# The last three groups of a gated MLP: down projections kept in PSUM, two more 4 KB places, loads spread out

## The chip, the cores and the metric

The kernel runs on one core of one Trainium2 chip. The metric is the device time of one execution in microseconds (us), by the median of several runs; less is better. All data is float32, and nearly all work is done on TensorE (PE in the profile), which multiplies a 128x128 stationary block by a moving block of up to 512 columns into PSUM. VectorE is DVE, ScalarE is ACT, GpSimd is POOL and SyncE is SP; PEld is the loading of stationary blocks, which overlaps PE.

## The reference, cut to what matters

A trunk of two layers over 256 positions of width 2048. Each layer is an attention mixer and then a gated MLP (the FFN) with a width of 5632 and a causal convolution of width 3 on the gate. The change touches the end of both FFNs.

```python
def _conv_ffn(h, w_up, w_conv, b_conv, w_down):
    u = h @ w_up
    gate, val = jnp.split(u, 2, axis=-1)
    gp = jnp.pad(gate, ((0, 0), (CONV_WIDTH - 1, 0), (0, 0)))
    acc = b_conv + gp[:, CONV_WIDTH - 1:CONV_WIDTH - 1 + S] * w_conv[CONV_WIDTH - 1]
    for j in range(CONV_WIDTH - 1):
        acc = acc + gp[:, j:j + S] * w_conv[j]
    return (jax.nn.silu(acc) * val) @ w_down

def _finish_layer(x, heads, w_o, norms, w_up, w_conv, b_conv, w_down):
    x = x + _rmsnorm(heads @ w_o, norms[1])
    f = _conv_ffn(_rmsnorm(x, norms[2]), w_up, w_conv, b_conv, w_down)
    return x + _rmsnorm(f, norms[3])
```

The output is x after both layers, 256 x 2048.

## The kernel before

**Numbers in two parts.** Every weight block of 128 x 2048 (1 MB, tile `raw`, three buffers) is loaded by an SP DMA in `piece` and split into a rounded part (`whi`, ACT, L557) and the rest (`wlo`, DVE, L558), four half-blocks of each. `mm3` (L118) forms a product by three matmuls: high by high, low by high, high by low.

**The FFN.** Its 5632 columns are eleven groups of 512. Groups 2, 4, 6 and 8 are "wide": `wide` uses a scheme of seven products with sums of weight blocks, which DVE makes in `sums` (d at L590, e at L591 and L592). The others are "narrow": sixteen-step products (`ws_tile`, L135 to L140), four such tiles for each pair of 256 columns, eight for a group. `keep` puts the activations of a group into two places of the pool `sh`. That pool has nine places of 4 KB per partition; it also holds d and e, the results of the down projections (y), loaded quarters of the memory tokens, and, through the whole FFN of layer 0, the memory keys of layer 1.

**Down projections.** A group's activations times `w_down` give four chunks of 512 columns (c = 0..3). `down(g, c)` loads one weight block, does 24 matmuls (12 for each half t of the positions) into a bank with tag "s", lets ACT copy each half to a place of `sh` (L701), and POOL sends it to `yout` in device memory, adding to what is there (L687 the first time, L689 later). Inside `wide`, one such down stands in each of the eight units of the loop, for the two groups before. After the last wide group (8), groups 9 and 10 are made; then eight downs follow for groups 8 and 9; then `yout` is read back into four places of `sh` (L788, `ys`). The eleventh group (g = 10) is done in PSUM: `evac` adds it to `ys` (L792), squares it (ACT, L205) and multiplies it by the gain (L796); when c = 3 is through, `rstd` follows (L198 on DVE, L200 on POOL), and `add_normed` adds four chunks to x (L489). In layer 1 the eleventh group runs half by half: all c for t = 0, then all c for t = 1, with the weights held in `h1` and `h2`; then SP stores the output (L978). In layer 0 it runs chunk by chunk, and `filler` (the values of memory for layer 1) follows.

**What sets the order.** `later(n, fn)` puts work into a list; each `ws_tile` and each `as_piece` takes one entry off (`step`). Below that the Tile layer schedules instructions of each engine and puts DMAs into the queue of the engine that issues them; a queue is in order, and an instruction waits there for its place in a pool to be free. The residual x is read back from device memory after the last wide group (L774, on POOL), and in layer 0 `late()` (`again` in `run`) also loads the four quarters of the memory tokens (`load_T`: SP at L248, then ACT L229 and DVE L230 four times each).

Of the kernel before, what the change touches and what calls it, by code (L numbers as in the profile page):

```python
# [30 lines left out]
COL_G = {"a0": 0, "a2": 16, "a4": 32, "b0": 48, "b2": 64, "b4": 80, "kv": 96}  # L31
# [4 lines left out]
GROUPS = DFF // 512  # L36
# [9 lines left out]
class Body:  # L46
# [16 lines left out]
        return self.sb.tile(shape, F32, name="sc", tag="sc", bufs=4)  # L63

    def sh(self, shape, dtype=F32):
        return self.sb.tile(shape, dtype, name="sh", tag="sh", bufs=9)

    def pairtile(self, dtype=F32):
        return self.sb.tile([P, 2, S], dtype, name="qk", tag="qk", bufs=5)
# [587 lines left out]
    def ffn(self, layer, h, each, filler=None, done=None, late=None):  # L657
        nc = self.nc
        up, uw, dn = (self.a["%s%d" % (k, layer)] for k in ("up", "uw", "dn"))
# [23 lines left out]
        acts = {}  # L683

        def out(g, c, part):
            if g == 0:
                nc.gpsimd.dma_start(yout[c], part)  # L687
            else:
                nc.gpsimd.dma_start(yout[c], part, accum_op=ALU.add)  # L689

        def down(g, c):


            parts = self.piece(dn[c, g])
            y = self.sh([P, 1024])
            yield
            for t in range(2):
                b = self.bank("s")
                self.as_mm([b, b], parts, acts[g], 0, (t,))
                yield  # L700
                self.pin(nc.scalar.copy(y[:, t * 512:(t + 1) * 512], b))  # L701
                if t:
                    out(g, c, y)
                else:
                    yield
# [29 lines left out]
        def narrow(g):  # L735
            for p in (2 * g, 2 * g + 1):
                w = p - 2 * sum(v < g for v in WIDE)
                ga = self.ws_pair(up[w, 0], h)
                if p == 0:

                    val = self.ws_pair(up[w, 1], h)
                Rb = spread().unsqueeze(1).to_broadcast([P, 2, S])
                nc.vector.tensor_tensor(ga, ga, Rb, op=ALU.mult)
                c = conv(p, ga)
                nc.vector.tensor_tensor(c, c, Rb, op=ALU.mult)
                if p:
                    val = self.ws_pair(up[w, 1], h)
                keep(p, c, val)

        def turned(g, made, i):  # L750

            both = []
            for of in made:
                b = self.bank("s")
                for j in range(2):
                    for t in range(2):
                        f = (2 * i + j) * P
                        nc.tensor.transpose(b[:, j * S + t * P:j * S + (t + 1) * P], of[t][:, f:f + P], self.ident)
                both.append(b.rearrange("p (j t) -> p j t", j=2))
            keep(2 * g + i, conv(2 * g + i, both[0]), both[1])  # L760
# [3 lines left out]
        before = [0, 1]  # L764
        forms = self.sb.tile([P, 4, 1024], F32R, name="x", tag="x", bufs=1)
        for g in WIDE:
            downs = [lambda b=b, c=c: down(b, c) for b in before for c in range(4)]
            made = self.wide(uw[WIDE.index(g)], h, s, forms, R[0], downs)
            for i in range(2):
                self.later(2 + i, lambda made=made, g=g, i=i: turned(g, made, i))  # L770
            if g == WIDE[-1]:
                self.x = self.sb.tile([P, 2, D], F32, name="x", tag="x", bufs=1)
                for t in range(2):
                    nc.gpsimd.dma_start(self.x[:, t, :], self.xout[t])  # L774
                if late:
                    late()
            narrow(g + 1)
            before = [g, g + 1]
        narrow(GROUPS - 1)
        for b in before:  # L780
            for c in range(4):
                for _ in down(b, c):
                    pass
        g = GROUPS - 1
        gs = [self.gain(2 * layer + 1, c) for c in range(4)]
        ys = [self.sh([P, 2, 512]) for _ in range(4)]
        for c in range(4):
# [2 lines left out]
        def evac(c, t, b):  # L790
            y = ys[c][:, t, :]
            nc.vector.tensor_add(y, y, b)  # L792
            self.square_into(y, ss[:, t, c:c + 1])
            if c == 3:
                r[t] = self.rstd(ss[:, t:t + 1, :])
            nc.vector.tensor_tensor(y, y, gs[c], op=ALU.mult)  # L796

        if not filler:

            banks = [[self.bank(), self.bank()] for _ in range(2)]  # L800
            banks += [[self.bank("s"), self.bank("s")] for _ in range(2)]
            store = self.stores("h1") + self.stores("h2")
            parts = [self.piece(dn[c, g], store=store[c]) for c in range(4)]
            for t in range(2):
                for c in range(4):
                    self.as_mm(banks[c], parts[c], acts[g], 0, (t,))
                    evac(c, t, banks[c][t])
                self.add_normed(ys, r[t], t, lambda c: done(t, c))
            return
        for c in range(4):  # L810
            b = self.as_chunk(dn[c, g:], acts[g])
            for t in range(2):
                evac(c, t, b[t])
        self.add_normed(ys, r[0], 0)
# [4 lines left out]
    def run(self):  # L819
        nc, a = self.nc, self.a  # L820
# [22 lines left out]
        b = self.bank("s")  # L843
# [65 lines left out]
        for j in range(12):  # L909
# [5 lines left out]
            if j % 3 == 2:  # L915
                i = j // 3
# [4 lines left out]
        lhs = [(mh[:, i, :], ml[:, i, :]) for i in range(4)] + [(dh[:, i, :], dl[:, i, :]) for i in range(4)]  # L921
# [11 lines left out]
        def again():  # L933
            self.memT = self.hset("h1")
            for i in range(4):
                self.load_T(a["memT"], COL_G["b4"], self.memT, i)

        self.ffn(0, h, lambda c: self.x_T(COL_G["kv"], hk, [c]), lambda: res.update(mv=self.mem_v(1)), late=again)
        mk, mv = res["mk"], res["mv"]

# [13 lines left out]
        def outs(hh):  # L954
            return heads[hh // 4][0][:, hh % 4, :], heads[hh // 4][1][:, hh % 4, :]
# [7 lines left out]
        hh, hl, _ = self.hset("h1")  # L963
        heads[2] = (hh[:, 0:4, :], hl[:, 0:4, :])
        lhs = [(mh[:, i, :], ml[:, i, :]) for i in range(4)] + [outs(i) for i in range(12)]
# [93 lines left out]

# [13 lines left out]
```

## Time and profile before

| | |
|---|---|
| runs | 2220.97 us median of 3 (2219.81 to 2222.61) |
| the profiled execution | 2222.25 us, of which the program's span is 2220.5 us |
| PE busy | 2190.2 us, 99% of the span, 11106 matmuls |
| PEld, DVE, ACT, POOL busy | 83%, 77%, 59%, 4% |
| granted TensorE clock | 9 tenths or more in all forty slices but the last (8) |
| moved by DMA | 479.04 MB, 216 GB/s in the mean |

In a row of the timeline stand the start, the duration, the engine, the line, the operation, the tiles and the count of merged instructions; in square brackets the idle time of the engine before it and what ended it. Matmuls are pipelined: one of 512 columns lasts 0.39 us in a row, and the next begins 0.23 us after it. So PE counts as busy nearly always, and what it loses stands in its few brackets.

### The profile page before, as it was taken

To read this page: it belongs to the slowest core of one execution; us is meant where nothing else is said; L and a number is where in the kernel's file an instruction comes from. 1 tells how busy PE (TensorE), PEld (TensorE's weight loads), DVE (VectorE), ACT (ScalarE), POOL (GpSimd) and SP (SyncE) were. 2 spreads that over 40 slices of the span, in tenths; PEclk is the share of its full clock that TensorE was granted. 3 is DMA by queue.
4 is the path that set the end of the run, shared out by engine and by line. 5 is a ranking of instruction groups with operands and counts; after the bars stand their busy time and mean duration, and the time that the engine had idled before them with its cause. 6 is when DMAs were issued, how large, how long until landed. Compare 5 with 4: busy or idle time off the path is not lost. (4 is left out here: it accounts for less than half of the span.)

```text
span 2220.5 us, 29136 instructions
## 1 busy us (share of the span) xinstructions
PE 2190.2 (99%) x11106; PEld 1846.8 (83%) x11106; DVE 1708.9 (77%) x2215; ACT 1313.2 (59%) x1870; POOL 93.8 (4%) x138
## 2 busy tenths in 40 slices
PE   9999999999999999999999999999999999999996
PEld 7888888888888888888788888878888888888885
DVE  6566767888888888886574677569989889898755
ACT  7545656566666666665564554456666666666553
POOL 0000000000000000000100000000000000000001
PEclk9999999999999999999999999999999999999998
DMA  8754555558586776875945444555676868778676
GB/s 321 267 178 159 196 182 210 182 207 262 194 252 198 245 229 208 272 259 192 282 172 190 152 171 168 193 190 190 236 237 199 254 192 256 218 231 259 227 214 187
DMA packets 76012, 479.04 MB, mean 216 GB/s; under 512 B 8672, under 2 KB 9056, under 8 KB 25312
## 3 DMA queue, kind: packets, MB, share of 16 engines
q1 hardware_dynamic: 60768, 418.45, 54.3%
q0 software_dynamic: 15104, 58.73, 11.7%
q8 instruction: 87, 1.43, 0.3%
q14 instruction: 53, 0.43, 0.1%
HBM read 428.91 MB, written 48.23 MB: 215 GB/s over the span
## 5 line engine op out<-in xcount | busy, mean ns | idle before, releaser
L558 DVE TENSOR_TENSOR wlo<-raw,whi 128x1024 fp32r<-128x1024 f32 (+1 forms) x758 | 879.3, 1174 | 324.7 <-ACT whi L557 313.7
L557 ACT CAST whi<-raw 128x1024 fp32r<-128x1024 f32 (+1 forms) x758 | 760.1, 1012 | 362.6 <-PE ps_g L118 132.9
L135 PE MATMUL ps_g<-h,whi 128*128 128x512 f32 x2640 | 942.4, 399 | 1.9 <-ACT whi L557 1.7
L136 PE MATMUL ps_g<-h,wlo 128*128 128x256 f32 x2816 | 760.7, 280 | 0.7 <-DVE wlo L558 0.7
L135 PEld LDWEIGHTS ps_g<-h,whi 128*128 128x128 f32 x2640 | 495.7, 188 | 116.3 <-ACT whi L557 2.2
L136 PEld LDWEIGHTS ps_g<-h,wlo 128*128 128x128 f32 x2816 | 531.3, 189 | 15.3 <-DVE wlo L558 1.0
L118 PE MATMUL ps_s<-whi,sh 128*128 128x512 f32 x1280 | 396.1, 391 | 0.0
L118 PEld LDWEIGHTS ps_s<-whi,sh 128*128 128x128 f32 x1280 | 240.4, 188 | 52.7
L118 PE MATMUL ps_s<-wlo,sh 128*128 128x512 f32 x640 | 252.3, 394 | 4.0 <-DVE wlo L558 4.0
L118 PE MATMUL ps_g<-whi,h 128*128 128x512 f32 x816 | 254.1, 392 | 0.8 <-ACT whi L557 0.8
L139 ACT COPY qk<-ps_g 128x256 f32<-128x256 f32 x160 | 59.6, 372 | 210.9 <-PE ps_g L138 210.8
L118 PEld LDWEIGHTS ps_g<-whi,h 128*128 128x128 f32 x816 | 152.7, 188 | 34.7 <-ACT whi L557 1.3
L701 ACT COPY sh<-ps_s 128x512 f32<-128x512 f32 x160 | 93.2, 582 | 130.3 <-PE ps_s L118 118.6
L558 DVE TENSOR_TENSOR x<-sh,x 128x1024 fp32r<-128x1024 f32 x128 | 156.0, 1222 | 15.8 <-ACT x L557 9.6
L118 PE MATMUL ps_g<-wlo,h 128*128 128x512 f32 x408 | 160.1, 393 | 0.2
L118 PEld LDWEIGHTS ps_s<-wlo,sh 128*128 128x128 f32 x640 | 120.2, 188 | 32.5 <-DVE wlo L558 6.5
L557 ACT CAST x<-sh 128x1024 fp32r<-128x1024 f32 x128 | 134.3, 1050 | 17.8 <-PE ps_s L118 16.4
L118 PE MATMUL ps_g<-whi,sh 128*128 128x512 f32 x368 | 115.5, 395 | 0.7 <-ACT whi L557 0.7
L140 DVE TENSOR_TENSOR qk<-ps_g,qk 128x256 f32<-128x256 f32 x160 | 67.3, 421 | 57.0 <-ACT qk L139 56.2
L118 PE MATMUL ps_g<-x,h 128*128 128x512 f32 x384 | 109.2, 392 | 0.0
L118 PE MATMUL ps_s<-x,h 128*128 128x512 f32 x384 | 108.5, 391 | 0.0
L689 POOL DMA_DIRECT2D yout<-sh x72 | 61.5, 855 | 1044.8 <-ACT sh L701 1034.5
(173 smaller groups left out, 1920.0 us busy)
## 6 DMA issues: line engine op xcount, KB each, us to landing
raw<-in_up_dram SPq DMA_DIRECT2D x112, 1024.0 KB, 4.9
raw<-in_dn_dram SPq DMA_DIRECT2D x88, 1024.0 KB, 4.9
raw<-in_uw_dram SPq DMA_DIRECT2D x64, 1024.0 KB, 7.1
yout<-sh POOLq DMA_DIRECT2D x80, 512.0 KB, 8.4
raw<-in_wqk_a_dram SPq DMA_DIRECT2D x24, 1024.0 KB, 4.9
raw<-in_wo_b_dram SPq DMA_DIRECT2D x16, 1024.0 KB, 4.9
raw<-in_wv_a_dram SPq DMA_DIRECT2D x12, 1024.0 KB, 4.8
raw<-in_wv_b_dram SPq DMA_DIRECT2D x12, 1024.0 KB, 4.8
```

Source lines behind the costliest of these rows:

```text
L118: mm = lambda *o, **k: self.pin(self.nc.tensor.matmul(*o, **k))
L135: mm(b, whi[:, ks], both, start=kt == 0, stop=False)
L136: mm(b[:, 0:S], wlo[:, ks], one, start=False, stop=False)
L139: nc.scalar.copy(out, b[:, S:])
L140: nc.vector.tensor_add(out, b[:, 0:S], out)
L557: self.pin(self.nc.scalar.copy(hi, of))
L558: self.pin(self.nc.vector.tensor_sub(lo, of, hi.bitcast(F32)))
L689: nc.gpsimd.dma_start(yout[c], part, accum_op=ALU.add)
L701: self.pin(nc.scalar.copy(y[:, t * 512:(t + 1) * 512], b))
```

## The change

1. Groups 8, 9 and 10 no longer pass through `yout`. In layer 1 the eight downs of groups 8 and 9 go straight into the eight banks that group 10 ends in; in layer 0 `as_chunk` runs each of the four chunks through twelve blocks of 128 rows instead of four. The matmuls and the weight blocks are the same; 16 ACT copies and eight accumulating DMAs of 512 KB go in each layer.
2. `sh` gets two more places (11). For them the scratch space of the software DMA queue is set to 8192 bytes per partition.
3. The two halves of x are put off by 5 and 8 steps, the four quarters of the memory tokens by 4, 7, 10 and 13.

```diff
-        return self.sb.tile(shape, dtype, name="sh", tag="sh", bufs=9)
+        return self.sb.tile(shape, dtype, name="sh", tag="sh", bufs=11)
...
                 for t in range(2):
-                    nc.gpsimd.dma_start(self.x[:, t, :], self.xout[t])
+                    self.later(5 + 3 * t, lambda t=t: nc.gpsimd.dma_start(self.x[:, t, :], self.xout[t]))
...
         narrow(GROUPS - 1)
-        for b in before:
-            for c in range(4):
-                for _ in down(b, c):
-                    pass
-        g = GROUPS - 1
+
+        last = before + [GROUPS - 1]
+        lhs = [p for b in last for p in acts[b]]
...
             store = self.stores("h1") + self.stores("h2")
-            parts = [self.piece(dn[c, g], store=store[c]) for c in range(4)]
+            for c in range(4):
+                for pi, b in enumerate(before):
+                    self.as_mm(banks[c], self.piece(dn[c, b]), lhs, pi)
+            parts = [self.piece(dn[c, GROUPS - 1], store=store[c]) for c in range(4)]
             for t in range(2):
                 for c in range(4):
-                    self.as_mm(banks[c], parts[c], acts[g], 0, (t,))
+                    self.as_mm(banks[c], parts[c], lhs, len(before), (t,))
                     evac(c, t, banks[c][t])
...
-            b = self.as_chunk(dn[c, g:], acts[g])
+            b = self.as_chunk(dn[c, last[0]:], lhs)
...
             for i in range(4):
-                self.load_T(a["memT"], COL_G["b4"], self.memT, i)
+                self.later(4 + 3 * i, lambda i=i: self.load_T(a["memT"], COL_G["b4"], self.memT, i))
...
-    nc = _bacc.Bacc("TRN2", target_bir_lowering=False, num_devices=1)
+    nc = _bacc.Bacc("TRN2", target_bir_lowering=False, num_devices=1, dynamic_dma_scratch_size=8192)
```

**Place 1: DVE in the first wide group of layer 0**, the sums of its third unit (d is `sh_4329`, e is `sh_4330`) and the start of the fourth (`sh_4409`). The semaphore DMASW6 here is that of the first transfer to `yout`. Before:

```order
L590 TENSOR_TENSOR sh_4329<-raw_4327 128x1024 [waits DMAHW2_49,DVE_49]
L591 TENSOR_TENSOR sh_4330<-raw_4327,sh_4329 128x512 [waits DMASW6_49,DVE_49]
L592 TENSOR_TENSOR sh_4330<-raw_4327,sh_4330 128x512 [waits DVE_49]
L558 TENSOR_TENSOR wlo_4335<-raw_4327,whi_4334 128x1024 [waits PE_49,Activation_49]
L558 TENSOR_TENSOR wlo_4337<-raw_4327,whi_4336 128x512 [waits PE_49,Activation_49]
L558 TENSOR_TENSOR wlo_4358<-raw_4355,whi_4357 128x1024 [waits DMAHW3_49,PE_49,Activation_49]
L558 TENSOR_TENSOR wlo_4362<-raw_4355,whi_4361 128x1024 [waits PE_49,Activation_49]
L558 TENSOR_TENSOR x_4186<-sh_4329,x_4186 128x1024 [waits PE_49,Activation_49]
L558 TENSOR_TENSOR x_4186<-sh_4330,x_4186 128x1024 [waits PE_49,Activation_49]
L590 TENSOR_TENSOR sh_4409<-raw_4407 128x1024 [waits DMAHW4_49,DVE_49]
```

After the change, the same instructions:

```order
L590 TENSOR_TENSOR sh_4329<-raw_4327 128x1024 [waits DMAHW2_49]
L591 TENSOR_TENSOR sh_4330<-raw_4327,sh_4329 128x512 [waits DVE_49]
L592 TENSOR_TENSOR sh_4330<-raw_4327,sh_4330 128x512 [waits DVE_49]
L558 TENSOR_TENSOR wlo_4335<-raw_4327,whi_4334 128x1024 [waits PE_49,Activation_49]
L558 TENSOR_TENSOR wlo_4337<-raw_4327,whi_4336 128x512 [waits PE_49,Activation_49]
L558 TENSOR_TENSOR wlo_4358<-raw_4355,whi_4357 128x1024 [waits DMAHW3_49,PE_49,Activation_49]
L558 TENSOR_TENSOR wlo_4362<-raw_4355,whi_4361 128x1024 [waits PE_49,Activation_49]
L558 TENSOR_TENSOR x_4186<-sh_4329,x_4186 128x1024 [waits PE_49,Activation_49]
L558 TENSOR_TENSOR x_4186<-sh_4330,x_4186 128x1024 [waits PE_49,Activation_49]
L590 TENSOR_TENSOR sh_4409<-raw_4407 128x1024 [waits DMAHW4_49,DMASW6_49]
```

The order is the same; the wait for the first transfer to `yout` has moved from e of the third unit to d of the fourth.

**Place 2: SP, the end of layer 0's FFN**, from the last down of a wide group on. Before:

```order
L98 DMA raw<-in_dn_dram 128x2048
L98 DMA raw<-in_up_dram 128x2048 x3
L248 DMA sh<-in_memT_dram 128x1024 x4
L98 DMA raw<-in_up_dram 128x2048 x13
L98 DMA raw<-in_dn_dram 128x2048 x12
```

After the change:

```order
L98 DMA raw<-in_dn_dram 128x2048
L98 DMA raw<-in_up_dram 128x2048 x8
L248 DMA sh<-in_memT_dram 128x1024 x2
L98 DMA raw<-in_up_dram 128x2048 x2
L248 DMA sh<-in_memT_dram 128x1024
L98 DMA raw<-in_up_dram 128x2048 x6
L248 DMA sh<-in_memT_dram 128x1024
L98 DMA raw<-in_dn_dram 128x2048 x12
```

The four quarters of the memory tokens stood together behind three weight loads; they now stand behind eight, ten and sixteen.

**Place 3: POOL, the end of layer 1.** Before:

```order
L689 DMA yout<-sh 128x1024 x28
L774 DMA x<-xout 128x2048 x2
L480 DMA sc<-in_gb_dram 128x512 x4
L689 DMA yout<-sh 128x1024 x7
L788 DMA sh<-yout 128x1024 x2
L689 DMA yout<-sh 128x1024
L788 DMA sh<-yout 128x1024 x2
L200 TENSOR_TENSOR small<-small,mhalf 128x1 x2
```

After the change:

```order
L687 DMA yout<-sh 128x1024 x4
L689 DMA yout<-sh 128x1024 x28
L774 DMA x<-xout 128x2048 x2
L480 DMA sc<-in_gb_dram 128x512 x4
L786 DMA sh<-yout 128x1024 x4
L200 TENSOR_TENSOR small<-small,mhalf 128x1 x2
```

The eight transfers to `yout` between the gains and the reading back are gone, and the four reads (L786 now) stand right behind the gains. The two halves of x stand next to each other in both.

## Rows read from the trace of the kernel before

**Rows 1.** Timeline, PE, first wide group of layer 0: ordinary spacing, then the stalls.

```profile
480.64 0.62 PE L118 MATMUL ps_g<-whi,h 128*128 128x512 f32 x2
481.10 0.39 PE L118 MATMUL ps_g<-wlo,h 128*128 128x512 f32 x1
...
488.21 0.62 PE L118 MATMUL ps_s<-whi,sh 128*128 128x512 f32 x2
489.81 0.50 PE L118 MATMUL ps_s<-wlo,sh 128*128 128x512 f32 x1 [0.98 <-DVE wlo L558]
...
620.27 0.50 PE L118 MATMUL ps_s<-wlo,sh 128*128 128x512 f32 x1 [0.81 <-DVE wlo L558]
...
881.28 0.50 PE L118 MATMUL ps_s<-wlo,sh 128*128 128x512 f32 x1 [0.94 <-DVE wlo L558]
```

**Rows 2.** Timeline, POOL and DVE, first wide group of layer 0.

```profile
477.55 0.58 POOL L687 DMA_DIRECT2D yout<-sh  x1 [90.73 <-ACT sh L701]
...
485.46 0.69 DVE L591 TENSOR_TENSOR sh<-raw,sh 128x512 f32<-128x512 f32 x1 [3.66 <-DMA yout<-sh]
...
493.08 1.22 DVE L590 TENSOR_TENSOR sh<-raw 128x1024 f32<-128x1024 f32 x1
```

**Rows 3.** Instructions on yout, whole run: who waited for it (us, times).

```profile
DVE sh L591: 15.8, 4
```

**Rows 4.** Timeline, ACT, DVE and PE, layer 0 after its last wide group.

```profile
942.71 6.52 ACT L229 ACTIVATE h<-sh,cols 128x256 fp32r<-128x256 f32 x16
...
948.42 5.62 DVE L230 SCALAR_TENSOR_TENSOR h<-sh,cols,h 128x256 fp32r<-128x256 f32 x14
...
966.44 1.05 ACT L557 CAST whi<-raw 128x1024 fp32r<-128x1024 f32 x1 [2.25 <-DMA raw<-in_up_dram]
...
972.23 0.49 PE L135 MATMUL ps_g<-h,whi 128*128 128x512 f32 x1 [1.75 <-ACT whi L557]
973.44 0.39 PE L136 MATMUL ps_g<-h,wlo 128*128 128x256 f32 x1 [0.71 <-DVE wlo L558]
```

**Rows 5.** Stretches of layer 1: length, PE, PEld, DVE, ACT, POOL busy, clock, DMA share, GB/s.

```profile
2040.00:2055.00 15.00, 15.00 (x81) 12.74 (x80) 13.09 (x16) 7.68 (x10) 1.95 (x3) 1.00 0.88 283
2055.00:2070.00 15.00, 15.00 (x93) 13.19 (x92) 12.83 (x23) 9.56 (x17) 2.13 (x4) 1.00 0.78 278
```

**Rows 6.** Timeline, DVE and PE, eleventh group of layer 0.

```profile
1091.03 0.69 DVE L792 TENSOR_TENSOR sh<-sh,ps_g 128x512 f32<-128x512 f32 x1 [7.17 <-DMA sh<-yout]
...
1093.46 0.74 PE L118 MATMUL ps_g<-whi,sh 128*128 128x512 f32 x2 [0.73 <-ACT whi L557]
1094.72 0.50 PE L118 MATMUL ps_g<-wlo,sh 128*128 128x512 f32 x1 [0.52 <-DVE wlo L558]
```

**Rows 7.** Timeline, PE, POOL and DVE, end of layer 1.

```profile
2186.24 5.66 PE L118 MATMUL ps_s<-h,sh 128*128 128x512 f32 x24
...
2196.36 0.53 POOL L788 DMA_DIRECT2D sh<-yout  x1 [5.29 <-DVE sh L796]
...
2197.33 5.66 PE L118 MATMUL ps_s<-h,sh 128*128 128x512 f32 x24
...
2200.08 0.69 DVE L792 TENSOR_TENSOR sh<-sh,ps_s 128x512 f32<-128x512 f32 x1 [0.28 <-DMA sh<-yout]
...
2202.82 2.74 DVE L489 SCALAR_TENSOR_TENSOR x<-sh,small,x 128x512 f32<-128x512 f32 x4 [0.46 <-POOL small L200]
2205.48 1.28 DVE L792 TENSOR_TENSOR sh<-sh,ps_g 128x512 f32<-128x512 f32 x2
...
2210.51 0.68 DVE L792 TENSOR_TENSOR sh<-sh,ps_s 128x512 f32<-128x512 f32 x1
```

**Rows 8.** Two stretches, PE alone: length, PE busy and matmuls, clock, DMA share, GB/s.

```profile
1425.00:1455.00 30.00, 30.00 (x132) 1.00 0.59 206
2140.00:2170.00 30.00, 30.00 (x133) 1.00 0.95 262
```

## The prediction

> **What bounds the kernel now.** I read the page first: PE is busy 99% of the span, so work taken from ACT, DVE, POOL or the DMA queues is worth nothing by itself. What can be won lies where PE stands still, or after its last matmul. The waits of PE and its timeline show where. The reader is to see three things. First, the ordinary spacing: three matmuls of 512 columns take 0.69 us, since two begin in the 0.46 us between 480.64 and 481.10 [rows 1]. Second, how a stall is priced: where the low part comes late, 1.60 us pass from 488.21 to 489.81 instead of 0.46, so 1.14 us are lost. The bracket says 0.98. The missing 0.16 is overlap: the matmul before a stall no longer runs into the next. So every stall costs its bracket plus 0.16. Third, the tail: PE's last matmul ends at 2202.99 (2197.33 + 5.66) [rows 7], and the span at 2220.5. In those 17.5 us no matmul runs.
>
> **The tail (layer 1).** The end is a chain on DVE that starts late. The last chunk of t = 0 has left PE at 2191.90 (2186.24 + 5.66), but its addition to `ys` starts at 2200.08, because the last read of `yout` was issued at 2196.36 only; POOL had waited for a free place in `sh` [rows 7]. From there on the order of DVE rules: 5.48 us from that addition to the end of the four updates of x (2202.82 + 2.74 = 2205.56), then 5.03 us from 2205.48 to the last addition of t = 1 at 2210.51, though PE had finished 7.52 us before it. From 2210.51 to the end it is a fixed 9.97 us (square, rstd, four updates, store).
>
> After the change `yout` is complete when the last wide group ends, and the four reads stand right behind the gains on POOL, long before they are needed. Then the chain follows PE. The last chunk of t = 0 is added at 2191.90, x is updated by 2197.38 (+ 5.48), the last addition of t = 1 could start at 2202.41 (+ 5.03), and PE gives it at 2202.99. So PE bounds it, with 0.58 us to spare, and the tail moves ahead by 2210.51 - 2202.99 = **7.52 us**. That is also its most; its least is 0, if the additions stay behind something else. I take 7.52, since each step is a row of the same instructions.
>
> **The stalls in the wide groups (layer 0).** In each of the four, e of the third unit needs a place of `sh` that an outgoing y holds until its transfer has landed: DVE stands 3.66 us until 485.46 for a transfer issued at 477.55 [rows 2], 15.8 us in four waits, all in layer 0 [rows 3], where the keys of layer 1 hold one of the nine places. The split is late by this, and PE stands 0.98, 0.81, 0.81 (a like one at 750.71) and 0.94 us [rows 1]: 3.54 + 4 x 0.16 = **4.18 us**. With eleven places the first wait for that transfer stands at d of the fourth unit, which starts at 493.08, while the transfer has landed by 485.46 [rows 2]: 7.6 us to spare. Layer 1 has nine places for the same work, and no such wait. Bounds 0 and 4.18; I take 4.18.
>
> **The burst after the last wide group (layer 0).** Sixteen ACT and fourteen DVE instructions for the memory tokens run in a row (6.52 and 5.62 us), while 2 MB of them and 2 MB of x load. The splits and with them the next weight loads are late; ACT waits 2.25 us for a weight block at 966.44, and PE stands 1.75 + 0.71 us [rows 4]: with two overlaps **2.78 us**. In layer 1 the same place has the 2 MB of x but no memory tokens, and PE is busy 15.00 of 15.00 us in both stretches [rows 5]. So it is the tokens that make the gap, and they now come one quarter at a time. Of x nothing is spread: the two halves follow each other on POOL without a wait between, as before. Bounds 0 and 2.78; I take 2.78.
>
> **The eleventh group of layer 0.** DVE waits 7.17 us for `ys`, and the splits queued behind it hold PE 0.73 + 0.52 us [rows 6]: with two overlaps **1.57 us**. Read that early, `ys` is there. Bounds 0 and 1.57; I take 1.57.
>
> **What is added.** The eight downs change their order of banks, from twelve matmuls on one to three by turns. Where chunks already run so, 132 matmuls fit in 30 us; where the downs run, 133 [rows 8]. One in 133 of 2 x 192 matmuls at 0.23 us is 0.66 us; counts are whole numbers, so the bounds are 0 and 0.7, and I take 0.3. The four reads of `yout` (2 MB) now fall right behind x and the gains, next to weight loads. The nearest price is the gap of the burst, 0 to 2.78 us a layer. I take 0: it brings transfers, but no work for ACT and DVE, and rows 5 show 283 GB/s without a stall. With more places three quarters of the tokens load together in the attention of layer 0, too; same bounds, same value, same reason. For the smaller scratch space of POOL's queue no row shows a price. If it made each transfer to `yout` wait for the one before, 7.9 us (477.55 to 485.46) would still fit in the time between two downs, as 493.08 is the next unit's d [rows 2]: I take 0, and the 4.18 us of the wide stalls as the upper bound. The copies and transfers that go lie beside PE and are worth nothing; that the DMA engines, 0.95 busy in the downs before [rows 8], get air only makes the splits safer.
>
> **Sum.** 7.52 + 4.18 + 2.78 + 1.57 - 0.3 = 15.75. The profiled execution took 2222.25, of which 15.75 leaves 2206.5. It lay 1.28 above the median of the runs (2220.97), so I predict 2205.2.
>
> **Rivals.**
> A. The reads of `yout` hurt the weight loads: the wait for `ys` turns into a wait for blocks in the narrow groups. For it: ACT waited 2.25 us for a block at 966.44 when 4 MB lay beside the weights [rows 4]. Against it: rows 5. Price 2.78 in one layer, 2208.0, or in both, 2210.8. The Trainium skill (DMA: Bandwidth & Descriptors, "Queues, rings and completion order") says that each DMA engine takes turns between the queues that have work, a packet at a time, so that a burst on POOL's queue slows SP's loads at once. The 2.25 us agree, and by that rule alone the price of A would be paid.
> B. The wide wait only moves to the next sum of a later unit: for it, that wait is still in the order; against it, 7.6 us to spare. The 4.18 stay: 2209.4.
> C. The spreading does not do what it says, since x still comes in one piece: the gap of layer 0 stays, 2208.0. Against it: layer 1's full PE beside the same x.
> D. The tail stays late, as the additions of t = 0 stand on DVE behind the last splits into `h2`: the sum without 7.52, 2212.7. Against it: the weight loads have the DMA engines more to themselves.
> E. Slower: a quarter of the tokens waits in SP's queue for its place in `sh`, and all weight blocks behind it wait as well. In rows 4 the late cast at 966.44 stopped PE at 970.48 (972.23 - 1.75), so 4.0 us of lead hide such a hold, and the rest falls on PE. A hold of 25 us would cost 21 us: 2226.2. It decides from a hold of 24 us on (15.75 + 4.4 + 4.0). Against it: the places that the quarters wait for are those of outgoing y's and of activations of groups 6 and 7, done when the wide group ends.
>
> **How the numbers follow.** Forecast 0.69 (2202.5 to 2208); A 0.10; B 0.06; C 0.05; D 0.04; E 0.03; nothing to be seen 0.03. About 0.2%, 4.4 us, is what a measurement of this kernel can tell. A to D are all faster than 2216.5, so faster has 0.94, the same 0.03 and slower 0.03. The range reaches from 2202.5, where the unknown costs are nothing and small stalls near by go too, to 2211, which takes in A, B and C.
>
> **What would show it.** In the profile after: no bracket of PE with DVE wlo in the wide groups of layer 0; none near the ninth and eleventh group of layer 0; the reads of `yout` landed long before the last downs; the last addition within 0.2 us of PE's last matmul, and the span ending about 10 us after it. New brackets of PE on whi or wlo in the narrow groups after the last wide one would speak for A or C; DVE still in L558 when the first chunk is done, for D; SP idle in front of L248, for E. If PE's stalls go but the time stays above 2211, the sum is wrong.

## The result, and the profile after

The changed kernel took 2205.34 us (median of 6 runs, 2204.65 to 2206.26) beside 2222.0 us of the kernel before (6 runs, 2219.81 to 2223.19): a ratio of 0.9926, 95% interval 0.9913 to 0.9939, or 16.7 us. The forecast was 2205.2. In three later batches the kernel before had 2224.26 (26 runs), 2223.1 (7 runs) and 2223.72 (23 runs, 2219.05 to 2229.87), and the changed kernel, beside the second, again 2205.35 (4 runs, 2204.9 to 2205.69), so the gain is nearer to 18 us. The times also lie closer together: the six runs of after 1.6 us, the six of before beside them 3.4, the 23 of before 10.8.

The profiled execution took 2204.65 us, its span 2202.9: 17.6 us less than before. I set the 11106 matmuls of the two traces side by side, one by one, and read where their starts drift apart:

| place | predicted | found |
|---|---|---|
| wide groups of layer 0, four stalls | 4.18 | 4.58 |
| after the last wide group of layer 0 | 2.78 | 2.81 |
| eleventh group of layer 0 | 1.57 | 2.18 |
| behind PE's last matmul | 7.52 | 8.81 |
| all other places | -0.3 | -0.75 |
| sum | 15.75 | 17.63 |

About half of the -0.75 lies ahead of the first wide group (0.27 of it in the first 20 us, where both kernels do the same), the rest in two places of layer 0 with 0.2 and 0.3 us; none lies in the downs of layer 1, for which the -0.3 stood.

All waits of PE that are left, by what released them: engine, line, releaser, us in total, times, longest.

```profile
PE ps_s L240 <- DVE x L489: 2.1, 1, 2.1
PE ps_s L846 <- DVE ones L840: 1.2, 1, 1.2
PE ps_g L118 <- ACT whi L557: 0.9, 1, 0.9
PE ps_s L240 <- DVE h L230: 0.5, 1, 0.5
PE ps_s L118 <- DVE wlo L558: 0.4, 2, 0.2
PE ps_g L135 <- DVE h L230: 0.2, 1, 0.2
```

None of the four places is in it: the 0.9 stands at 13.79, the 0.4 is two waits of 0.2, and the 2.1 is the transposing of x behind layer 1's attention; before has all three too. In the first wide group, timeline of POOL, DVE and PE (the rows that answer to [rows 1, 2]):

```profile
477.56 0.58 POOL L687 DMA_DIRECT2D yout<-sh  x1 [90.41 <-ACT sh L701]
...
480.93 1.21 DVE L590 TENSOR_TENSOR sh<-raw 128x1024 f32<-128x1024 f32 x1
482.18 0.69 DVE L591 TENSOR_TENSOR sh<-raw,sh 128x512 f32<-128x512 f32 x1
...
490.83 1.22 DVE L590 TENSOR_TENSOR sh<-raw 128x1024 f32<-128x1024 f32 x1
```

```profile
488.59 0.62 PE L118 MATMUL ps_s<-whi,sh 128*128 128x512 f32 x2
489.05 0.39 PE L118 MATMUL ps_s<-wlo,sh 128*128 128x512 f32 x1
```

The sum e (L591) starts 0.04 us after d's end (480.93 + 1.21) instead of 3.66 us, since its place is free; d of the fourth unit, which now holds the wait, starts at 490.83 without a bracket. PE takes 0.46 us from the high to the low part, where [rows 1] show 1.60.

After the last wide group, PE alone (length, PE busy and matmuls, clock, DMA share, GB/s), first before, then after:

```profile
970.00:980.00 10.00, 7.54 (x42) 1.00 0.54 191
```

```profile
960.00:970.00 10.00, 10.00 (x59) 1.00 0.95 309
970.00:980.00 10.00, 10.00 (x59) 1.00 0.95 361
```

The eleventh group's first three additions on DVE, after:

```profile
1077.90 0.69 DVE L790 TENSOR_TENSOR sh<-sh,ps_g 128x512 f32<-128x512 f32 x1 [0.67 <-PE ps_g L118]
...
1081.50 0.68 DVE L790 TENSOR_TENSOR sh<-sh,ps_g 128x512 f32<-128x512 f32 x1
...
1094.38 0.69 DVE L790 TENSOR_TENSOR sh<-sh,ps_g 128x512 f32<-128x512 f32 x1 [0.67 <-PE ps_g L118]
```

PE is full although more is loaded (361 GB/s for 191), and the additions wait for PE or for nothing, not 7.17 us for `ys` [rows 6]. The end, DVE and PE (against [rows 7]):

```profile
2183.11 0.69 DVE L790 TENSOR_TENSOR sh<-sh,ps_s 128x512 f32<-128x512 f32 x1 [0.53 <-PE ps_s L118]
...
2185.87 2.74 DVE L489 SCALAR_TENSOR_TENSOR x<-sh,small,x 128x512 f32<-128x512 f32 x4 [0.46 <-POOL small L200]
...
2188.51 5.66 PE L118 MATMUL ps_s<-h,sh 128*128 128x512 f32 x24
...
2194.20 0.69 DVE L790 TENSOR_TENSOR sh<-sh,ps_s 128x512 f32<-128x512 f32 x1 [0.52 <-PE ps_s L118]
...
2196.93 2.74 DVE L489 SCALAR_TENSOR_TENSOR x<-sh,small,x 128x512 f32<-128x512 f32 x4 [0.44 <-POOL small L200]
```

The last addition of each half waits about 0.5 us for PE. The very last starts at 2194.20, 0.03 us after PE's last matmul ends (2188.51 + 5.66 = 2194.17); before it was 7.52 us late.

### The profile page after: what moved, and what is told of

It reads as the page before. It is cut to its first block, busy times and chain, and to the rows that moved or that the text cites. A ratio compares the mean times of both kernels' runs of the same rounds, so it can differ in the third digit from the quotient of the medians.

```text
span 2202.9 us, 29043 instructions
## 1 busy us (share of the span) xinstructions
PE 2188.7 (99%) x11106; PEld 1848.0 (84%) x11106; DVE 1713.0 (78%) x2215; ACT 1297.1 (59%) x1838; POOL 79.9 (4%) x122
## 4 chain that ended last, share of the span: by engine, by line
PE 98%; issue 1%; DVE 1%; DMA 0%; ACT 0%; SPq 0%; POOLq 0%; POOL 0%; DVEq 0%; ACTq 0%
PE ps_g L135 28%; PE ps_g L118 26%; PE ps_s L118 23%; PE ps_g L136 15%; PE ps_g L138 2%; PE ps_s L758 1%; PE ps_s L240 1%; DMA raw<-in_wmv_dram 0%; PE ps_s L291 0%; PE ps_s L318 0%; DVE wlo L558 0%; PE ps_s L397 0%; PE ps_s L354 0%; PE ps_s L455 0%; PE ps_s L415 0%
## 5 line engine op out<-in xcount | busy, mean ns | idle before, releaser
L118 PE MATMUL ps_s<-whi,sh 128*128 128x512 f32 x1088 | 336.6, 391 | 0.0
L118 PE MATMUL ps_g<-whi,h 128*128 128x512 f32 x816 | 254.1, 392 | 0.9 <-ACT whi L557 0.9
L118 PEld LDWEIGHTS ps_s<-whi,sh 128*128 128x128 f32 x1088 | 204.4, 188 | 45.2
L118 PE MATMUL ps_s<-wlo,sh 128*128 128x512 f32 x544 | 214.3, 394 | 0.4 <-DVE wlo L558 0.4
L118 PEld LDWEIGHTS ps_g<-whi,h 128*128 128x128 f32 x816 | 152.7, 188 | 34.8 <-ACT whi L557 1.3
L118 PE MATMUL ps_g<-whi,sh 128*128 128x512 f32 x560 | 174.8, 393 | 0.0
L118 PE MATMUL ps_g<-wlo,h 128*128 128x512 f32 x408 | 160.2, 393 | 0.2
L557 ACT CAST x<-sh 128x1024 fp32r<-128x1024 f32 x128 | 134.4, 1050 | 17.4 <-PE ps_s L118 16.4
L701 ACT COPY sh<-ps_s 128x512 f32<-128x512 f32 x128 | 74.4, 581 | 106.0 <-PE ps_s L118 106.0
L118 PEld LDWEIGHTS ps_g<-whi,sh 128*128 128x128 f32 x560 | 104.8, 188 | 22.1
L118 PEld LDWEIGHTS ps_s<-wlo,sh 128*128 128x128 f32 x544 | 102.2, 188 | 23.2 <-DVE wlo L558 1.3
L118 PE MATMUL ps_g<-wlo,sh 128*128 128x512 f32 x280 | 109.8, 392 | 0.0
L118 PE MATMUL ps_g<-x,h 128*128 128x512 f32 x384 | 109.2, 392 | 0.0
```

The lines of the kernel that those rows point to most:

```text
L118: mm = lambda *o, **k: self.pin(self.nc.tensor.matmul(*o, **k))
L557: self.pin(self.nc.scalar.copy(hi, of))
```

## The experiments

**Layer 1 alone.**

```diff
 # kernel before, nine places
-        for b in before:
+        if filler:
+            for b in before:
...
+            for c in range(4):
+                for pi, b in enumerate(before):
+                    self.as_mm(banks[c], self.piece(dn[c, b]), lhs, pi)
...
-                    self.as_mm(banks[c], parts[c], acts[g], 0, (t,))
+                    self.as_mm(banks[c], parts[c], lhs, len(before), (t,))
```

> The kernel before with the PSUM accumulation of the last three groups in layer 1 alone; nine places, loads as before, layer 0 as before. Theory (the tail is late because the last read of yout is late; PE's stalls in layer 0 are separate): the tail after PE's last matmul shrinks from 17.5 us to between 8.7 and 10.0, the stalls of layer 0 stay, and the time falls by 7.5 to 8.8 us to some 2214. Rival (the early reads need the two more places): the fourth read finds no place until the ninth group's activations are free, and the tail stays above 13 us, time over 2217. Rival (the gain is the copies and transfers that went): no place in the profile stands out, gain about half of the whole 16.7 us.

2218.27 us (8 runs) beside 2224.26 (26 runs); ratio 0.997 (0.996 to 0.9981), 6.7 us by that ratio and 6.0 by the medians, short of the 7.5 to 8.8 expected, and a time that the first rival gives as well (over 2217). The trace decides between the two. The last addition waits for PE:

```profile
2209.03 0.69 DVE L794 TENSOR_TENSOR sh<-sh,ps_s 128x512 f32<-128x512 f32 x1 [0.52 <-PE ps_s L118]
```

So the mechanism holds: the tail behind the last matmul is 9.37 us, 8.13 less than in the first profile of before. The first rival is right that the fourth read finds no place at first (it is issued at 2181.40, and PE L118 ended its wait), but that is early enough; and one place of the profile stands out, against the second. The gain is smaller because that profile had the longest tail of those with the old end. In the four others with nine places and the old end the last addition came 5.03 to 7.46 us after PE's last matmul (5.73 in the second look at before). My estimate from these: the mean of the five, 6.3, and the 0.7 by which the program's end is shorter here (last section) make 7.0, near the 6.0 to 6.7 measured.

**Eleven places alone.**

```diff
-        return self.sb.tile(shape, dtype, name="sh", tag="sh", bufs=9)
+        return self.sb.tile(shape, dtype, name="sh", tag="sh", bufs=11)
...
+    ... dynamic_dma_scratch_size=8192
```

> The kernel before with eleven places in sh and the smaller scratch space, nothing else. Theory: the four stalls of PE in the wide groups of layer 0 go (4.2 by the sum, 4.6 by the aligned traces), the gap of the burst (2.6 to 2.8 us) and the one in the eleventh group (1.6 to 2.2 us) stay, and the tail shortens by no more than 0.5 us, since the reads of yout still wait for its last transfers: 2217 to 2218. Rival (the wait only moves to another sum): 2222, the brackets at another unit. Rival (places alone bring most of the change): under 2212.

2218.28 (7 runs); 0.9969 (0.9957 to 0.9981), 6.9 us by the ratio and 6.0 by the medians, more than the 4.2 to 4.7 expected (and the time just above the 2217 to 2218). Matmul by matmul the four stalls give 4.58, as the whole change gives there; both rivals fall. The rest I don't ascribe: the profile is of the fastest of the seven runs (2211.56, the others 2214.57 to 2219.56), and in it the gap after the last wide group and the eleventh group's are each 0.9 us shorter and the tail 5.7, where at most 0.5 was expected. The last addition is 3.12 us late, less than in any old end with nine places, and the last transfer to `yout` is issued 17.4 us before PE's last matmul ends (13.3 to 15.3 with nine). So the places may give some of the tail too; one profile doesn't settle it. That they do not remove it fits what ends the wait of the last read there:

```profile
2186.95 0.53 POOL L788 DMA_DIRECT2D sh<-yout  x1 [4.45 <-DMA yout<-sh]
```

It waits for the last transfer to `yout` to land, and for no place.

**Nine places in the changed kernel** (the counterpart).

> The changed kernel with nine places and the scratch space of before. Theory (the places matter in the wide groups alone, since the reads of yout find room as soon as activations are read): the four stalls in the wide groups of layer 0 come back, 4.2 to 4.6 us, and the rest stays: 2209.5 to 2210.5. Rival (the early reads need the places): the eleventh group of layer 0 stalls again and the tail grows, 2213 or more.

2210.35 (4 runs), 5.0 us more than the changed kernel; the forecast of 2209.5 to 2210.5 was hit. DVE and PE again have the old rows:

```profile
485.28 0.69 DVE L591 TENSOR_TENSOR sh<-raw,sh 128x512 f32<-128x512 f32 x1 [2.88 <-DMA yout<-sh]
```

```profile
489.62 0.50 PE L118 MATMUL ps_s<-wlo,sh 128*128 128x512 f32 x1 [0.42 <-DVE wlo L558]
...
619.99 0.50 PE L118 MATMUL ps_s<-wlo,sh 128*128 128x512 f32 x1 [0.72 <-DVE wlo L558]
...
750.76 0.50 PE L118 MATMUL ps_s<-wlo,sh 128*128 128x512 f32 x1 [1.11 <-DVE wlo L558]
...
881.18 0.50 PE L118 MATMUL ps_s<-wlo,sh 128*128 128x512 f32 x1 [0.79 <-DVE wlo L558]
```

Brackets of 3.04 and 4 x 0.27 (0.16 of lost overlap and 0.11 behind each stall, as the next section shows) are 4.12; at PE's last matmul the two traces are 4.05 apart. The tail is 8.71 us, so the rival falls. Together the two runs show that the places, not the accumulation, remove this term.

**The smaller scratch space alone.**

```diff
+    ... dynamic_dma_scratch_size=8192   # kernel before, nine places
```

> The kernel before with the scratch space of the software DMA queue set to 8192 bytes per partition, nothing else. Theory: nothing waits for that space; the time is that of before within 1 us, and the transfers to yout land after 8.4 us in the median as before. Rival (POOL waits for room): longer times from issue to landing or a later issue on POOL, and the time rises by up to 4 us.

2223.36 (10 runs) beside 2224.26; 0.9996 (0.9987 to 1.0005): no change that can be measured, as expected. The transfers land after 8.5 us in the median, 8.4 before. In the trace it shortens the program's last step by 1.32 us (below).

**The spreading alone.**

```diff
+                    self.later(5 + 3 * t, ...)     # x, kernel before
...
+                self.later(4 + 3 * i, ...)         # memory tokens
```

> The kernel before with the loads of memory tokens and x spread, nothing else. Theory (the tokens' loads and their sixteen ACT and DVE instructions make the gap after the last wide group of layer 0): that gap of PE, 2.46 us in brackets, goes, the others stay: 2219 to 2219.5. Rival (x makes the gap, and x comes in one piece as before): the gap stays and the time is 2222.

2220.51 (10 runs); 0.9984 (0.9975 to 0.9993), 3.6 us (1.6 to 5.6) for the 2.5 to 3 expected; the time itself is above the 2219 to 2219.5 expected, as the kernel before had 2224.26 beside it and not 2222. PE has no gap at the place, so the rival falls. Without the two lines for x the program has the same order of instructions on every engine, so none of this is x's: it is the tokens', as the prediction said.

**No spreading in the changed kernel.** This was the surprise.

```diff
-                    self.later(5 + 3 * t, lambda t=t: nc.gpsimd.dma_start(self.x[:, t, :], self.xout[t]))
+                    nc.gpsimd.dma_start(self.x[:, t, :], self.xout[t])
...
-                self.later(4 + 3 * i, lambda i=i: self.load_T(a["memT"], COL_G["b4"], self.memT, i))
+                self.load_T(a["memT"], COL_G["b4"], self.memT, i)
```

> The changed kernel with the loads of memory tokens and x in one burst, as before the change. Theory (the tokens make the gap): the gap of PE after the last wide group of layer 0 comes back, 2.6 to 2.8 us: about 2208. Rival (with eleven places the burst does no harm): no gap, 2205.3.

2210.38 (4 runs): 5.0 us lost, not 2.7. POOL, ACT and PE point to a first cause, and stretches of all engines show a second (length, PE, PEld, DVE, ACT, POOL busy, clock, DMA share, GB/s):

```profile
954.35 2.20 POOL L786 DMA_DIRECT2D sh<-yout  x4
```

```profile
964.02 1.05 ACT L557 CAST whi<-raw 128x1024 fp32r<-128x1024 f32 x1 [3.57 <-DMA raw<-in_up_dram]
```

```profile
969.82 0.80 PE L135 MATMUL ps_g<-h,whi 128*128 128x512 f32 x1 [2.95 <-ACT whi L557]
971.03 0.58 PE L136 MATMUL ps_g<-h,wlo 128*128 128x256 f32 x1 [0.41 <-DVE wlo L558]
```

```profile
965.00:970.00 5.00, 2.05 (x11) 1.42 (x10) 4.37 (x9) 5.00 (x10) 0.00 (x0) 0.90 0.66 274
970.00:975.00 5.00, 4.58 (x13) 3.54 (x14) 4.98 (x5) 0.28 (x1) 0.00 (x0) 0.50 0.59 198
975.00:980.00 5.00, 5.00 (x28) 4.40 (x27) 2.06 (x3) 2.37 (x3) 0.00 (x0) 0.92 0.81 252
```

The reads of `yout` are issued 0.11 us after the weight block that ACT then waits for; the block takes 9.7 us to land (954.24 to 963.95), where it took 8.3 before. ACT waits 3.57 us instead of 2.25 [rows 4], and PE stands 4.10 us with the overlaps, in two stops of which the first is 3.2. In the gap the granted clock falls to 0.50, the lower of its two levels (1.2 GHz), and the 15 matmuls behind the gap begin nearly twice as far apart (0.43 us for 0.23 where there are 512 columns), 2.2 us more. 4.1 + 2.2 is the 6.24 by which this trace falls behind the changed kernel's here, to 0.1.

**The same, with the reads of `yout` held back in layer 0.**

```diff
         for c in range(4):
+            if filler:
+                nc.vector.tensor_copy(ys[c][:, 0, :2], acts[before[1]][2][0][:, :2].bitcast(F32))
             nc.gpsimd.dma_start(ys[c].rearrange("p t n -> p (t n)"), yout[c])
```

> The changed kernel with the loads of tokens and x at once, as before, and with the four reads of yout in layer 0 held back until the activations of group 9 are ready (a copy of two columns into each place makes the transfer wait). With the loads at once but the reads early, ACT waited 3.57 us for a weight block, PE stood 3.2 us, a clock of 0.5 followed, and the median was 2210.4. My theory: 2 MB of reads of yout beside the tokens, x and the gains are what made the wait longer than the 1.3 to 2.3 us of the kernels without them; held back, PE stands about 2 us, the clock stays at 1.00, and the time is 2207.5 to 2208.5. Rival: the run of thirty ACT and DVE instructions for the tokens alone delays the splits and so the next block; then the reads do not matter and the time stays at 2210.

2207.76 (6 runs, 2206.05 to 2209.63), inside the 2207.5 to 2208.5 expected. The reads are issued at 1014.47, the block lands in 7.6 us, and POOL, ACT, PE and the stretch (PE alone) read:

```profile
1014.47 2.34 POOL L788 DMA_DIRECT2D sh<-yout  x4 [60.40 <-ACT whi L557]
```

```profile
961.66 1.05 ACT L557 CAST whi<-raw 128x1024 fp32r<-128x1024 f32 x1 [1.58 <-DMA raw<-in_up_dram]
```

```profile
967.45 0.49 PE L135 MATMUL ps_g<-h,whi 128*128 128x512 f32 x1 [1.08 <-ACT whi L557]
968.66 0.39 PE L136 MATMUL ps_g<-h,wlo 128*128 128x256 f32 x1 [0.72 <-DVE wlo L558]
```

```profile
970.00:980.00 10.00, 10.00 (x59) 1.00 0.80 309
```

ACT waits 1.58 us and not 3.57, so the rival falls, and the clock stays. So the loads of the tokens in one piece cost 2.4 us (2207.76 - 2205.35; 2.2 by the ratios to the kernel before), and the early reads beside them 2.0 to 2.6 more, with this run and the next. The single times overlap a little: two of these six runs lie above 2209, and the nine runs with the early reads go from 2208.89 to 2212.36.

**No spreading, a second time.**

> The changed kernel with the loads of tokens and x at once, a second time. My theory: PE stands over 3 us at 970, the clock is then at half for some 5 us, and the time is 2210 as the first time. Rival: the clock's fall was chance, and it does not come in this profile; then 2208.

2209.74 (5 runs), as expected. PE stands 3.22 us, and the clock falls again:

```profile
970.00:980.00 10.00, 10.00 (x51) 0.83 0.85 297
```

**Layer 0's accumulation alone.**

```diff
 # kernel before, nine places
-        for b in before:
+        if not filler:
+            for b in before:
...
-            b = self.as_chunk(dn[c, g:], acts[g])
+            b = self.as_chunk(dn[c, last[0]:], lhs)
```

> The kernel before, with the accumulation in PSUM of the last three groups in layer 0 alone (nine places, nothing spread, layer 1 as before). My theory: only the wait of DVE for ys in the eleventh group goes, and PE's two stalls there (1.58 us in the profile before, 2.18 with what is near) do not come back, while the four stalls of the wide groups, the gap after the last wide group and the tail behind PE's last matmul stay: about 2221.5 to 2222.5 where the kernel before has 2223 to 2224. Rival: without the two added places the reading of yout waits for places that outgoing y's or the tokens hold and DVE waits for ys as before; no change.

2222.75 (12 runs) beside 2223.72; 0.9996 (0.9987 to 1.0005), just outside the 2221.5 to 2222.5 expected. The stalls of the eleventh group are gone (2.18 us by the matmuls), so the rival falls. But no gain can be measured, and in the profile the gap after the last wide group did not stay as it was: the price of the early reads is paid there. Two of them are issued from 961.99 on, the block of 961.86 takes 9.5 us, and PE stands 4.09 us:

```profile
971.44 1.05 ACT L557 CAST whi<-raw 128x1024 fp32r<-128x1024 f32 x1 [3.45 <-DMA raw<-in_up_dram]
```

The clock falls here too (0.89 and 0.94 in the next two stretches of 10 us). By itself this part shows no gain; in the changed kernel, where the loads are spread, neither the gap nor the stalls are there.

**A second look at the kernel before.**

> The kernel before, a second look. My theory: the gap after the last wide group and the tail behind PE's last matmul differ from run to run (the gap 2 to 3 us without and 6 us with a fall of the clock; the tail 14 to 17.5 us), which is where the 2219.6 to 2228.8 of its times come from, while the four wide stalls come back with 0.8 to 1.7 us each. Rival: the gap and the tail are as in the first profile within 0.3 us, and the spread has another source.

2224.56 (12 runs). The tail is 15.71 us in place of 17.50, the third wide stall 1.63 in place of 0.97, and the stretch after the gap reads:

```profile
970.00:980.00 10.00, 8.32 (x37) 0.83 0.43 147
```

The gap and the tail do differ from run to run, as expected; with the fall of the clock the gap costs 3.7 us here, not 6. The rule that I had in mind for the clock does not hold, though. Of nine profiles with a gap at this place the clock fell in five (PE stood 4.1, 4.1, 3.2, 3.0 and 2.1 us) and stayed in four (2.9, 2.2, 2.2, 1.9). The longest gaps all had it, but so had the 2.1 us of this second look. What decides there stays open.

**The last update of x on two other engines**, to shorten the tail further.

```diff
+            if pool and c == 3:
+                self.nc.scalar.activation(ys[c][:, t, :], ys[c][:, t, :], AF.Copy, scale=r)
+                self.nc.gpsimd.tensor_tensor(xs, ys[c][:, t, :], xs, op=ALU.add)
+                continue
```

> The changed kernel with the last of the four updates of x for t = 1 at the very end taken from DVE: ACT multiplies by rstd, POOL adds to x. Theory (the tail is one chain: addition, square, rstd, four updates of 0.69 us on DVE, store): if ACT and POOL together need under 2.1 us, DVE's chain is one update shorter and the span 0.5 to 0.7 us; if POOL's addition takes longer than 1.5 us, nothing is won or up to 1 us is lost. Rival (the end is set by the stores): no change within 0.2 us either way.

2206.48 (4 runs), about 1.1 us worse than the changed kernel, as the expectation has it for an addition of over 1.5 us on POOL. POOL and DVE:

```profile
2198.51 1.74 POOL L491 TENSOR_TENSOR x<-sh,x 128x512 f32<-128x512 f32 x1 [0.83 <-ACT sh L490]
```

```profile
2197.72 3.08 DVE L493 SCALAR_TENSOR_TENSOR x<-sh,small,x 128x512 f32<-128x512 f32 x3 [0.44 <-POOL small L200]
```

Three updates on DVE take 3.08 us beside POOL's addition, where four take 2.74 alone: the last of the three lasts 1.75 us instead of 0.75. The Trainium skill (Trainium Architecture — The Big Picture, "What this means for kernel authors") says that DVE and GpSimd contend for a shared port, as an exclusive lock. This trace agrees that they contend (the slow update runs from 2199.05 to 2200.80, and POOL's addition beside it ends at 2200.25); whether as a lock, no run here shows.

**The changed kernel again.**

> The changed kernel itself, timed again beside the next ones: 2205 to 2206, and a span whose tail after PE's last matmul is between 8.7 and 10.0 us. Theory: of the 1.27 us by which the tail came out shorter than its sum, all lies after the last store has landed, and it differs from run to run; so this profile's tail need not be 8.7 again.

2205.35 (4 runs); 0.9915 (0.99 to 0.993). Its matmuls follow those of the first profile within 0.9 us, most of it at the start and where x is transposed behind layer 1's attention; there the granted clock is 0.83 in 1470 to 1480, where the first profile has 1.00. The tail is 8.70 us, so the theory that its end differs from run to run is wrong: from the landing of the last store to the end it is 1.03 us in both.

## Why the prediction was right, point by point

- **The tail: right in its mechanism, 1.3 us too small in size.** The chain follows PE with 0.52 us to spare (0.58 predicted). The step that failed is "from 2210.51 to the end it is a fixed 9.97 us". After it is 8.66. From the last addition to the landing of the last store both have 7.6; what shrank is the program's end behind that, 2.35 to 1.03 us (next section). The 7.52 itself held for that one profile; with nine places and the old end the others were 5.0 to 7.5 us late. What held the last read of `yout` back is also not quite what the prediction says. It names a free place in `sh`; but in the first profile the last transfer to `yout`, whose sum the read needs, lands at 2195.81, only 0.07 us before the DVE instruction that ends the wait in [rows 7] (2195.88), and in two others (the second look at before, then the spreading alone) the transfer ended the wait:

```profile
2196.95 0.53 POOL L788 DMA_DIRECT2D sh<-yout  x1 [4.26 <-DMA yout<-sh]
2195.40 0.54 POOL L788 DMA_DIRECT2D sh<-yout  x1 [4.83 <-DMA yout<-sh]
```

  So a free place alone would not have cured the tail, as the run with eleven places shows (3.12 us late); taking the last transfers out did.
- **The wide stalls: right, 4.58 for 4.18.** The wait moved to d of the fourth unit and cost nothing there, as the 7.6 us of room said; rival B does not occur. The 0.4 that is missing is in the price of a stall. The prediction adds 0.16 to each bracket; but the late matmul itself also runs longer (0.50 us for 0.39), and the one behind it begins 0.34 us later and not 0.23:

```profile
489.81 0.50 PE L118 MATMUL ps_s<-wlo,sh 128*128 128x512 f32 x1 [0.98 <-DVE wlo L558]
490.15 0.39 PE L118 MATMUL ps_s<-whi,sh 128*128 128x512 f32 x1
```

  So a stall here costs its bracket plus 0.27, and 3.54 + 4 x 0.27 is 4.62. The size is that of one execution: the four stalls of the second look at before were 0.98 to 1.63 us each, without the 0.11.
- **The burst: right in cause, and the price without its cover was too low.** That it is the tokens and not x was right; rival C does not occur. 2.78 fits the first profile and the 2.4 us of the unspread loads with the reads held back, but leaves out the clock's fall, which came in five of nine profiles and made the cost 3.7 to 6.2 us there.
- **The eleventh group: right, 2.18 for 1.57.** Here too each stop costs 0.27 beyond its bracket, and a third one, of 0.08, stands behind the two: 0.73 + 0.52 + 0.08 + 3 x 0.27 = 2.14.
- **The reads of `yout` at nothing: right in the sum, with a reason that is not enough.** "It brings transfers, but no work for ACT and DVE" would have held for the unspread kernel too, and there the reads cost 2.0 to 2.6 us. What hides them is the spreading. Each read now waits for a place that a quarter of the tokens leaves (the wait ends with DVE h L230), so in layer 0 POOL issues them at 973.56, 975.14, 986.64 and 1018.69 instead of together behind the gains. Rival A's price was real, and the rule of the Trainium skill beside it (DMA: Bandwidth & Descriptors, "Queues, rings and completion order") agrees where the loads fall together: 7.3 to 8.4 us for the block in six profiles without the reads, 8.6 to 9.7 in three with them. In the changed kernel a block beside the tokens took 9.0 us (959.54 to 968.57), and no instruction of ACT waited for one there.
- **The order of banks: 0.3 predicted, nothing found.** Layer 1's downs after the change have the same 132 and 133 matmuls in 30 us as [rows 8] (length, PE, PEld, DVE, ACT, POOL busy, clock, DMA share, GB/s):

```profile
2130.00:2160.00 30.00, 30.00 (x133) 24.62 (x132) 15.35 (x14) 13.57 (x14) 0.00 (x0) 1.00 0.56 188
2140.00:2170.00 30.00, 30.00 (x132) 24.61 (x131) 18.34 (x16) 15.77 (x16) 0.00 (x0) 1.00 0.60 210
```

- **The scratch space at 0** held by a run of its own, and **the tokens in the attention of layer 0 at 0** by the traces: from 20 to 470 us they drift apart by 0.07. **D** and **E** did not occur: the first addition of the tail waits for PE, and PE has no wait beside the tokens' loads.

That the time came out within 0.2 us is luck. The sum was 1.9 us too small against its own profile, and it was taken from a median of three runs, 2220.97, that was low against the 2222.0 of six and the later 2223.1 to 2224.6; the two errors cancel.

## What to carry to other kernels

Read which wait ends last before pricing a cure: here a free place and a landing transfer ended within 0.07 us of each other, and only one of the two was named. Price a transfer at nothing only after asking what will load beside it and how much lead the next weight block has then: the same reads were free behind spread loads and cost 2 us and more beside a burst. A stall of PE can cost more than its bracket: 0.27 us more here at the full clock, and 1 to 3 us more where the matmuls behind it ran at the lower one. So look at the granted clock in the microseconds after a gap. Parts of a change need not add up: here the early reads of layer 0 showed no gain alone and stood free only where the loads beside them were spread.

## What the runs showed of the hardware

At the program's end POOL drains its queue (a DRAIN instruction behind the last line, in the trace's sequencer records). It starts 5.9 us before the last store lands, and where it takes longer it sets the end:

| kernels | transfers issued by POOL | scratch space | DRAIN, us | last store landed to end, us |
|---|---|---|---|---|
| before (two profiles), before with loads spread | 112 | as set without the argument | 7.46 | 2.33 to 2.35 |
| accumulation in one layer (two kernels) | 104 | the same | 6.80, 6.81 | 1.65, 1.67 |
| changed, nine places | 96 | the same | 6.15 | 1.05 |
| before with 8192 bytes | 112 | 8192 | 2.72 | 1.03 |
| changed | 96 | 8192 | 3.46 | 1.03 |

Without the argument every transfer less takes off 0.08 us ((7.46 - 6.15) / 16). With 8192 bytes the DRAIN ends before the last store has landed and costs nothing; why 96 then take longer than 112 stays open (with POOL's addition just ahead of it, in the run with two other engines, it took 4.27). This is the 1.3 us that the tail gave beyond its term.
